# A hybrid decoder layer on one core: elementwise work moved from POOL to VectorE, two copies to ScalarE, and a new order of the heads' stage

## The chip, the cores and the metric

The kernel runs on one core of one Trainium2 chip. Five engines work side by side, each through its own queue of instructions in order: PE (TensorE) multiplies matrices, DVE (VectorE), ACT (ScalarE) and POOL (GpSimd) do elementwise work, and SP issues the transfers between HBM and the on-chip memory. The metric is the device time of one execution in microseconds (us). Engines wait for one another through semaphores, and the profile names for each wait what ended it.

## The reference, cut to what matters

The program is one layer on 1024 tokens plus 16 learned meta tokens, with 1024 channels. The part that the change touches is the mixer in the middle of the layer: four recurrent heads, and four groups of channels that are pooled over windows of 2, 4, 8 and 16 tokens.

```python
u = rmsnorm(h, mix_norm_pre[l])
proj = u @ w_in[l]
q, f_logit, i_in, g_out, v_pool, gate_a, gate_b = jnp.split(proj, cuts, axis=-1)
a = hgrn2(q, f_logit, i_in, g_out, lbs[l], hgrn_out_norm[l])
p = multiscale_pool(v_pool, pool_proj[l], pool_scale[l])
z = (jax.nn.sigmoid(gate_a) * (a @ w_branch_hgrn[l])
     + jax.nn.sigmoid(gate_b) * (p @ w_branch_pool[l]))
...
# hgrn2: f = lb + (1-lb) sigmoid(f_logit), k = (1-lb) sigmoid(-f_logit); per head and chunk of tokens
#   scores[t,s] = sum_k q[t,k] * prod(f[s+1..t],k) * k[s,k]   (s <= t)
#   o = scores @ v + (q * prod f) @ state,  state' = (prod f) * state + (k * rest of f)^T @ v
#   o is normalised per head and multiplied by sigmoid(g)
# multiscale_pool: mean over the trailing window minus the token, times a 128x128 matrix per group
```

After the mixer follow an output projection, a norm, and a gated MLP with a causal convolution. All of it is float32; the kernel splits each float32 operand into a high and a low part and makes three matrix products of them.

## The kernel before, in words

Channels lie on the 128 partitions and tokens along the free dimension. The program runs in stages: the input norm and the value projection, the other projections of the two gates and of f and q (these by a seven-product scheme, and their results go to HBM scratch: fscr, kscr, kbscr, qscr, sscr), then the heads' stage, then the branch products BB and BA, the output projection, and the MLP.

The heads' stage is the one that changes. `ORDER` writes it out by hand as a list of steps in which the engines' queues are built: `h0` to `h3` is the next step of a head, `PV0` to `PV3` the projection of a pooling group (`PVa`, `PVb` its first and second half of the contraction, names ppv), `sp` the end of the pooling of a group, `G2` and `G3` two gate projections (pg), `PP` the 128x128 product of a group (ppp), `sa` the splitting of a head's output, `w` the preparing of later weights. A tile framework then places the instructions on each engine's queue from that list; inside a queue nothing overtakes.

A head (`head_steps`) loads f, q, kb and k from scratch (L655 to L658), then builds the scores within chunks of 128 tokens by doubling: for each level 1, 2, 4 ... 64 PE multiplies k and q blocks (names sb and sl, L690, L696, L719), and VectorE grows k (L673), q (L677, L679, first step L714) and f (L681) by one level. A level's products wait for the growth of the level before it, and the growth waits for the products that still read k and q. VectorE copies the scores from PSUM: masked for small levels (L711, L721), plainly for the two large ones (L705, into sc). Then k is transposed (pt), the state increments are multiplied (ds), VectorE runs along the states (st, L768), PE multiplies the outputs (po, L785, L786), and a norm with ScalarE's logarithm and exponential (L796, L797) follows, for which the square is split into rh and rl (L836).

A weight of a projection is loaded to wraw (L147), ScalarE casts the high part (whi, L150), and another engine subtracts to get the low part (wlo, L151). There are three buffers of each of wraw, whi and wlo, and the loader runs three weights ahead (`AHEAD`), so a cast waits until PE has done with the weight three before. After a projection `post_pv` copies it to vp and makes the window sum by one to four additions of shifted rows (L818), and `pool_split` divides, subtracts and splits it (L830, plh, pll).

`POOLED` names the operations that go to POOL instead of VectorE: the first growth of k of each head (uk1), the splits of the weights of PV0 to PV3, G2, G3 and PP2, and one rl. The window sums run on POOL too. Loads of a head are issued on SP's queue after the weight load that was last created before them in the program (`tc.issue_after(stage["load"].ins)`).

Of the kernel before, what the change touches and what calls it, by code (L numbers as in the profile page):

```python
# [12 lines left out]
ALU = mybir.AluOpType  # L13

P = 128
D = 1024
SEQ = 1024
NM = 16
L = SEQ + NM
# [33 lines left out]
ZA = 4  # L53
AHEAD = 3

ORDER = ("h0 h1 PVa0 h0 h1 PVb0 h0 h1 h0 PVa1 h1 h0 sp0 PVb1 h1 h0 h1 PVa2 sp1 h0 h1 PVb2 h0 h1 h2 h0 PVa3 sp2 h1 h0 h1 h3 "
         "PVb3 h0 h1 h2 Ga2 sp3 h0 h1 h2 h3 Gb2 h2 h3 sa0 PP0 PP1 h2 h3 Ga3 h2 h3 h2 Gb3 h3 h2 h3 PP2 PP3 h2 h3 sa1 h2 h3 w0 w1 "
         "BB0 w4 h2 h3 w4 BB1 h2 h3 BB2 sa2 h3 BB3 w5 BB4 sa3 w4 w5 BB5 w5 BB6 BB7 w5 BA0 w2 BA1 w3 BA2 BA4 BA3 BA5 BA6 BA7")
POOLED = ("uk1.0 uk1.1 uk1.2 uk1.3 wBA2 wBA6 wBA7 wBB2 wPP2 wPV0 wPV1 wPV2 wPV3 wG2 wG3 "
          "rsl.0").split()  # L60
TRUNC = False

CH_ALL = [(0, 348), (348, 346), (694, 346)]
# [4 lines left out]
def trunk_kernel(ctx: ExitStack, tc: tile.TileContext, x, meta_tokens, mix_norm_pre,  # L68
# [3 lines left out]
    nc = tc.nc  # L72
    act, dve, pool_e, pe = nc.scalar, nc.vector, nc.gpsimd, nc.tensor
# [6 lines left out]
    stage = {}  # L80
# [13 lines left out]
    def nm(s):  # L94
        cnt[0] += 1
        return f"{s}_{cnt[0]}"

    def slot(n, dtype=F32, name="s"):
        return stage["fm", "p"].tile([P, n], dtype, tag="fm", name=nm(name), padded_shape=[P, LP])
# [17 lines left out]
    def small(shape, name, tag, bufs=4):  # L117
        return sm.tile(shape, F32, tag=tag, name=nm(name), bufs=bufs)
# [95 lines left out]
    class Strassen:  # L214

        ORDER = ("P1", "P2", "P6", "P5", "P3", "P7", "P4")
        MOVING = dict(P1="b11", P2="b21", P3="b22", P4="t4", P5="t1", P6="t2", P7="t3")
        SECOND = ("P3", "P5", "P7")

        def __init__(self, units, run, early, quarters, base, halo, put, whole):  # L220
# [6 lines left out]
            for u in run:  # L227
                self.seq += [(u, p) for p in self.ORDER if u >= early or p not in ("P1", "P2")]
            self.got, self.at, self.kept, self.begun = [], 0, [], {}
# [328 lines left out]
    vmd = dram.tile([NM, 512], F32, name="vmscr")  # L558
# [49 lines left out]
    def eng(op):  # L608
        return pool_e if op in POOLED else dve

# [39 lines left out]

    def head_steps(h):
        f, k, kb, q = slot(NM + L, name="f"), slot(NM + L, name="k"), slot(NM + L, name="kb"), slot(NM + L, name="q")
        vmeta = small([NM, P], "vmeta", "vmeta", 2)
        with tc.issue_after(stage["load"].ins):
            nc.sync.dma_start(f, fdr[h])  # L655
            nc.sync.dma_start(q[:, NM + T0 :], qdr[h])
            nc.sync.dma_start(kb[:, M0:], kbdr[h])
            nc.sync.dma_start(k, kdr[h])  # L658
            nc.sync.dma_start(vmeta, vmd[:, h * P : (h + 1) * P])
        yield  # L660
        pool_e.memset(f[:, NM - 1 : NM], 1.0)
        pool_e.memset(k[:, NM - 1 : NM], 0.0)
# [36 lines left out]
        def level_out(lv, ps):  # L699
            if lv >= SB:  # L700
                o3 = sc.rearrange("p (c t) -> p c t", c=NCH)
                p3 = ps[:, : NCH * lv].rearrange("p (c h) -> p c h", c=NCH)
                for i in range(P // (2 * lv)):
                    n = 2 * lv * i
                    dve.tensor_copy(o3[n : n + lv, :, n + lv : n + 2 * lv], p3[n : n + lv])  # L705
                return
            o4 = near.rearrange("p (c b two h) -> p c b two h", c=NCH, two=2, h=lv)[:, :, :, 1, :]
            p4 = ps[:, : NCH * SB // 2].rearrange("p (c b h) -> p c b h", c=NCH, h=lv)
            nb = SB // (2 * lv)
            m4 = masks[lv].rearrange("p (o b h) -> p o b h", o=1, h=lv).to_broadcast([P, NCH, nb, lv])  # L710
            dve.copy_predicated(o4, m4, p4)  # L711
# [12 lines left out]
        for lv in LEVELS:  # L724
            if lv == NM:
                pm = bank("sm")
                for i in range(HALO):
                    pe.matmul(pm[:NM, i : i + 1], k[:, i * NM : (i + 1) * NM], q[:, NM + T0 + i : NM + T0 + i + 1],
                              start=True, stop=True)
                act.copy(scm, pm[:NM, :HALO])  # L730
            ps = level_mm(lv)
            grow(lv)
            level_out(lv, ps)
            if lv == SB // 2:
                for n in range(0, P, SB):
                    act.copy(sc.rearrange("p (c t) -> p c t", c=NCH)[n : n + SB, :, n : n + SB], n3[n : n + SB])
            yield

        heads[h]["v"] = slot(NCH * P, name="vh")
        with tc.issue_after(stage["load"].ins):  # L740
            nc.sync.dma_start(heads[h]["v"].rearrange("p (c v) -> p c v", c=NCH),
                              vd[:, :, h * P : (h + 1) * P].rearrange("c p v -> p c v"))
        kt = slot(NCH * P, name="kt")
# [62 lines left out]
    def post_pv(g, pv):  # L806
        w = POOL_WINDOWS[g]
        vp, s1 = slot(L, name="vp"), slot(L, name="s1")
        s2 = slot(L, name="s2") if w > 2 else None
        for (lo, n), ps in zip(CH_ALL, pv):  # L810
            act.copy(vp[:, lo : lo + n], ps[:, :n])
        cur, step = vp, 1
        bufs = [s1, s2]
        while step < w:
            nxt = bufs[0]
            bufs = bufs[::-1]
            a = 2 * step - 1
            pool_e.tensor_tensor(nxt[:, a:L], cur[:, a:L], cur[:, a - step : L - step], ALU.add)  # L818
            cur, step = nxt, 2 * step
        pooled[g] = (cur, vp)  # L820

# [70 lines left out]
    def job(kind, i):  # L892
        if kind == "G":
            return (wblock(WIN, 0, KD, CG + i * P, P), KD, u_q, CH_Q, lambda r: post_g(i, r))
        if kind == "PV":
            return (wblock(WIN, 0, KD, CV + i * P, P), KD, u_all, CH_ALL, lambda r: post_pv(i, r))
        if kind == "PP":
            return (pool_proj[0, i].rearrange("(k c) d -> c k d", k=1), 1,
                    lambda k, lo, n: (pin[i][0][:, lo : lo + n], pin[i][1][:, lo : lo + n]), CH_Q,
                    lambda r: post_pp(i, r))  # L900
        if kind == "BA":
            return (wblock(w_branch_hgrn[0], 0, HEADS, i * P, P), HEADS, a_x, CH_Q, lambda r: post_branch(sas, i, r))
        return (wblock(w_branch_pool[0], 0, HEADS, i * P, P), HEADS, p_x, CH_Q, lambda r: post_branch(sbs, i, r))
# [4 lines left out]
    BEGUN = [(e, p) for es in ((0, 1), (2, 3, UP0)) for p in ("P1", "P2") for e in es]  # L908
    KEPT = BEGUN + [(u, p) for u in (0, UP0) for p in Strassen.ORDER[2:]]
    kept = [[dram.tile([P, 1024], F32, name=f"kept{t}{h}") for h in "hl"] for t in range(len(KEPT) // 2)]  # L910
# [54 lines left out]

    order = ORDER.split()
    order = [(o_[:-1], int(o_[-1])) for o_ in order]
# [23 lines left out]
    def gate_steps(d):  # L991
# [10 lines left out]
        else:  # L1002
# [19 lines left out]
    gates = Strassen([(WIN, dict(F=CF, Q=CQ, A=CA, B=CB)[k] + 2 * P * j) for k, j in GUNITS], range(len(GUNITS)),  # L1022
                     EARLY, gq, NM, ghalo, put_gate, lambda u, i: None)
# [116 lines left out]
    for kind, i in order:  # L1140
# [9 lines left out]
        if kind == "h":  # L1150
            if i not in gens:
                gens[i] = head_steps(i)
            next(gens[i], None)
            continue
# [36 lines left out]
    for name, names in (("v1", ("b11h", "b11l", "b21h", "b21l")), ("v2", ("b22h", "b22l", "t1h", "t1l"))):  # L1191
        n, o = (HP, HO) if name == "v1" else (HN, 0)
# [584 lines left out]
```

## Time and profile before

| | us |
|---|---|
| median of three runs | 1337.31 (1335.11 to 1337.34) |
| the profiled execution | 1336.16 |
| its span, first to last instruction | 1334.5 |
| PE busy | 1292.2 |
| VectorE busy | 972.5 |
| ScalarE busy | 519.0 |
| POOL busy | 405.2 |

The page gives per engine the time that it was busy and the number of its instructions. A group of instructions has a line of the kernel, an engine, an operation, the tile written and the tiles read, the count, the busy time, the mean of one, and the idle time of the engine just before, with what ended it. The granted clock of PE stands beside stretches of time as a share of full speed; its mean over the span is 0.988. A wait is put down to the engine that ended it last.

### The profile page before, as it was taken

The page shows a single profiled execution, that of the slowest core. Times are in us where ns is not written, and L with a number is a line of the kernel's source. Part 1 is how long each engine was busy: PE and PEld are TensorE (multiplying, and loading weights), DVE is VectorE, ACT ScalarE, POOL GpSimd, SP SyncE. Part 2 cuts the span into 40 slices and gives each one's busy share as a digit, 9 for nine tenths or more (in the row PEclk, how much of TensorE's full clock was granted, in tenths as well). Part 3 has the DMA queues.
Part 4 walks back from the last instruction along what each step waited for, and adds up shares of the span by engine and source line. Part 5 has one row for each costly group of instructions (what it writes and reads, how often), then busy time and mean ns, then how long its engine had stood idle before and what let it go on. Part 6 is the DMA issues. An engine that isn't in the chain of part 4 may idle for free.

```text
span 1334.5 us, 21944 instructions
## 1 busy us (share of the span) xinstructions
PE 1292.2 (97%) x8617; PEld 1143.3 (86%) x8617; DVE 972.5 (73%) x1287; ACT 519.0 (39%) x891; POOL 405.2 (30%) x325
## 2 busy tenths in 40 slices
PE   8999999999789879999999999999999999999997
PEld 6799899999788779987899888888888888888886
DVE  6768965542786976686668999888988885455757
ACT  5554433333125445224664222222222223454543
POOL 3015333322354100052026555446556652000000
PEclk9999999999899889999999999999999999999999
DMA  8135643334232276887686777776767799676644
GB/s 271 41 109 178 199 136 103 111 119 146 92 114 100 65 253 191 305 286 248 225 301 225 209 206 191 201 205 152 180 164 148 178 244 301 216 230 223 221 173 158
DMA packets 143802, 247.62 MB, mean 186 GB/s; under 512 B 11000, under 2 KB 75164, under 8 KB 143698
## 3 DMA queue, kind: packets, MB, share of 16 engines
q1 hardware_dynamic: 131634, 221.83, 49.4%
q0 software_dynamic: 12064, 24.38, 10.9%
q8 instruction: 68, 1.11, 0.3%
q14 instruction: 36, 0.29, 0.1%
HBM read 174.11 MB, written 95.09 MB: 202 GB/s over the span
## 4 chain that ended last, share of the span: by engine, by line
PE 62%; DVE 0%; issue 0%; ACT 0%; DMA 0%; DVEq 0%
PE P L305 11%; PE P L304 11%; PE P L307 11%; PE pd L184 5%; PE pd L185 5%; PE pd L186 5%; PE pm L184 2%; PE pm L185 2%; PE pm L186 2%; PE pba L204 1%; PE pba L205 1%; PE pba L208 1%; PE pbb L204 1%; PE pbb L205 1%; PE pbb L208 1%; PE pt L1271 1%
## 5 line engine op out<-in xcount | busy, mean ns | idle before, releaser
L305 PE MATMUL P<-v,whi 128*128 128x512 f32 (+2 forms) x408 | 140.7, 353 | 0.0
L304 PE MATMUL P<-v,whi 128*128 128x512 f32 (+2 forms) x408 | 140.7, 352 | 0.0
L307 PE MATMUL P<-v,wlo 128*128 128x512 f32 (+2 forms) x424 | 135.1, 349 | 0.0
L275 POOL TENSOR_TENSOR swa<-wraw,wraw 128x512 f32<-128x512 f32 x32 | 48.5, 1516 | 192.1 <-DMA wraw<-in_w_in_dram 98.7
L249 ACT CAST whi<-wraw 128x512 fp32r<-128x512 f32 x90 | 53.1, 618 | 102.3 <-PE P L305 75.7
L1511 DVE TENSOR_TENSOR rot<-wraw,rot 128x1024 fp32r<-128x1024 f32 x31 | 38.0, 1224 | 72.2 <-ACT rot L1510 72.2
L304 PEld LDWEIGHTS P<-v,whi 128*128 128x128 f32 x408 | 76.7, 188 | 10.4
L305 PEld LDWEIGHTS P<-v,whi 128*128 128x128 f32 x408 | 76.6, 188 | 10.2
L307 PEld LDWEIGHTS P<-v,wlo 128*128 128x128 f32 x424 | 74.1, 188 | 10.8
L185 PE MATMUL pd<-rot 128*128 128x512 f32 x272 | 82.1, 389 | 0.0
L186 PE MATMUL pd<-rot 128*128 128x512 f32 x272 | 82.1, 389 | 0.0
L184 PE MATMUL pd<-rot 128*128 128x512 f32 x272 | 81.1, 389 | 0.1
L250 DVE TENSOR_TENSOR wlo<-wraw,whi 128x512 fp32r<-128x512 f32 x86 | 77.4, 922 | 2.7 <-ACT whi L249 2.7
L250 DVE TENSOR_TENSOR wlo<-swb,whi 128x512 fp32r<-128x512 f32 x64 | 67.6, 1064 | 9.7 <-ACT whi L249 9.6
L249 ACT CAST whi<-swa 128x512 fp32r<-128x512 f32 x64 | 38.1, 618 | 92.6 <-PE P L305 77.4
L304 PE MATMUL P<-uhi,whi 128*128 128x258 f32 (+2 forms) x240 | 68.6, 303 | 0.0
L305 PE MATMUL P<-ulo,whi 128*128 128x258 f32 (+2 forms) x240 | 68.4, 303 | 0.0
L1510 ACT CAST rot<-wraw 128x1024 fp32r<-128x1024 f32 x31 | 32.7, 1054 | 90.7 <-PE pd L186 89.4
L249 ACT CAST whi<-swb 128x512 fp32r<-128x512 f32 x64 | 38.1, 618 | 70.9 <-PE P L305 61.5
L304 PE MATMUL P<-t2h,whi 128*128 128x258 f32 (+2 forms) x228 | 65.2, 304 | 0.3 <-DVE sg L864 0.3
L304 PE MATMUL P<-t4h,whi 128*128 128x258 f32 (+2 forms) x228 | 65.5, 304 | 0.0
L305 PE MATMUL P<-t4l,whi 128*128 128x258 f32 (+2 forms) x228 | 65.3, 304 | 0.0
(383 smaller groups left out, 3884.9 us busy)
## 6 DMA issues: line engine op xcount, KB each, us to landing
wraw<-in_w_in_dram SPq DMA_DIRECT2D x36, 512.0 KB, 4.8
yt<-ysum SPq DMA_DIRECT2D x33, 512.0 KB, 5.4
wraw<-in_ffn_w_gate_dram SPq DMA_DIRECT2D x26, 512.0 KB, 5.9
wraw<-in_ffn_w_up_dram SPq DMA_DIRECT2D x22, 512.0 KB, 6.5
wsum<-in_ffn_w_down_dram SPq DMA_DIRECT2D x22, 512.0 KB, 8.5
wraw<-in_w_out_dram SPq DMA_DIRECT2D x18, 512.0 KB, 5.1
ysum<-ys SPq DMA_DIRECT2D x11, 768.0 KB, 5.6
sa<-sscr SPq DMA_DIRECT2D x16, 513.0 KB, 4.4
```

What stands on the lines that cost most here:

```text
L184: pe.matmul(ps, ahi, bhi, start=first, stop=False)
L185: pe.matmul(ps, ahi, blo, start=False, stop=False)
L186: pe.matmul(ps, alo, bhi, start=False, stop=last)
L204: pe.matmul(ps[:, :n], whi[:, k, :], xhi, start=(k == 0), stop=False)
L249: act.copy(hi, src)
L250: (pool_e if 4 <= i < 2 * self.early else dve).tensor_tensor(lo, src, rr(hi), ALU.subtract)
L275: pool_e.tensor_tensor(s1, a21, a22, ALU.add)
L304: pe.matmul(d, whi[:, k, :], xh[:, c : c + w], start=(k == 0 and onto is None), stop=False, **go)
L305: pe.matmul(d, whi[:, k, :], xl[:, c : c + w], start=False, stop=False, **go)
L307: pe.matmul(x[:, o : o + w], wlo[:, k, :], xh[:, c : c + w], start=False, stop=(k == 3), **go)
L1510: act.copy(hi, src)
L1511: dve.tensor_tensor(lo, src, rr(hi), ALU.subtract)
```

## The change

All operations in `POOLED` and the window sums go from POOL to VectorE. The copies of the two large levels from PSUM to sc (L705) go from VectorE to ScalarE. The loads of heads 0 and 1 are tied to the last weight load of the stage before (`gates.loaded`) instead of the last projection weight; the small load of vmeta moves from the head's first step to the one that loads its values. `ORDER` puts the whole of PV0 and the first half of PV1 ahead of the second step of heads 0 and 1, and shifts the halves of the later projections by some places.

```diff
-ORDER = ("h0 h1 PVa0 h0 h1 PVb0 h0 h1 h0 PVa1 h1 h0 sp0 PVb1 h1 h0 h1 PVa2 sp1 h0 h1 PVb2 h0 h1 h2 h0 PVa3 sp2 h1 h0 h1 h3 "
-         "PVb3 h0 h1 h2 Ga2 sp3 h0 h1 h2 h3 Gb2 h2 h3 sa0 ...
+ORDER = ("h0 h1 PV0 PVa1 h0 h1 PVb1 h0 h1 h0 PVa2 h1 sp0 h0 h1 PVb2 h0 h1 sp1 h0 h1 h2 PVa3 h0 h1 sp2 h0 h3 "
+         "PVb3 h1 h0 h1 h0 h1 h2 Ga2 sp3 h0 h1 h2 h3 Gb2 h2 h3 sa0 ...
-POOLED = ("uk1.0 uk1.1 uk1.2 uk1.3 wBA2 wBA6 wBA7 wBB2 wPP2 wPV0 wPV1 wPV2 wPV3 wG2 wG3 "
-          "rsl.0").split()
+POOLED = ()
...
     def head_steps(h):
-        vmeta = small([NM, P], "vmeta", "vmeta", 2)
-        with tc.issue_after(stage["load"].ins):
+        with tc.issue_after((stage["load"] if h >= 2 else gates.loaded).ins):
             nc.sync.dma_start(f, fdr[h])
...
-            nc.sync.dma_start(vmeta, vmd[:, h * P : (h + 1) * P])
...
-                    dve.tensor_copy(o3[n : n + lv, :, n + lv : n + 2 * lv], p3[n : n + lv])
+                    act.copy(o3[n : n + lv, :, n + lv : n + 2 * lv], p3[n : n + lv])
...
         heads[h]["v"] = slot(NCH * P, name="vh")
+        vmeta = small([NM, P], "vmeta", "vmeta", 2)
         with tc.issue_after(stage["load"].ins):
+            nc.sync.dma_start(vmeta, vmd[:, h * P : (h + 1) * P])
...
     def post_pv(g, pv):
-            pool_e.tensor_tensor(nxt[:, a:L], cur[:, a:L], cur[:, a - step : L - step], ALU.add)
+            dve.tensor_tensor(nxt[:, a:L], cur[:, a:L], cur[:, a - step : L - step], ALU.add)
```

The framework places the rest. Lines of the changed kernel stand one to three lower in number than those of the one before in this part. Three places in the queues:

SP's queue around the first loads of heads 0 and 1; wraw_3580 (now 3486) is PV3's weight, wraw_3857 (now 3663) G2's, sscr stores are results of the gates. Before:

```order
L147 DMA wraw_3389<-in_w_in_dram 128x8x128
L659 DMA vmeta_3399<-vmscr 16x128
L659 DMA vmeta_3409<-vmscr 16x128
L871 DMA sscr<-sg_3263 128x514
L147 DMA wraw_3580<-in_w_in_dram 128x8x128
L871 DMA sscr<-sg_3321 128x512
L147 DMA wraw_3857<-in_w_in_dram 128x8x128
L871 DMA sscr<-sg_3340 128x512
L655 DMA f_3395<-fscr 128x1056
L656 DMA q_3398<-qscr 128x1026
```

Now:

```order
L146 DMA wraw_3389<-in_w_in_dram 128x8x128
L870 DMA sscr<-sg_3263 128x514
L146 DMA wraw_3486<-in_w_in_dram 128x8x128
L870 DMA sscr<-sg_3321 128x512
L146 DMA wraw_3663<-in_w_in_dram 128x8x128
L870 DMA sscr<-sg_3340 128x512
L653 DMA f_3395<-fscr 128x1056
L654 DMA q_3398<-qscr 128x1026
```

The two loads of vmeta are gone from here; the head's loads keep their place behind both weights.

VectorE's queue at the first levels of heads 0 (f_3395) and 1; sl_3592 (now 3677) is head 0's product of level 2, wlo_3666 the low part of G2's weight, s the window sums. Before:

```order
L714 TENSOR_TENSOR q_3408<-q_3408,f_3405 128x512
L681 TENSOR_TENSOR f_3395<-f_3395 128x528
L677 TENSOR_TENSOR q_3408<-q_3408,f_3405 128x1024
L721 COPY_PREDICATED near_3502<-mbase,sb_3507 128x256
L673 TENSOR_TENSOR k_3396<-k_3396,f_3395 128x264x2
L679 TENSOR_TENSOR q_3398<-q_3398,f_3395 128x256x2
L711 COPY_PREDICATED near_3457<-mask_145,sl_3592 128x64x2
```

Now:

```order
L674 TENSOR_TENSOR q_3406<-q_3406,f_3403 128x1024
L718 COPY_PREDICATED near_3585<-mbase,sb_3590 128x256
L678 TENSOR_TENSOR f_3395<-f_3395 128x528
L678 TENSOR_TENSOR f_3403<-f_3403 128x528
L150 TENSOR_TENSOR wlo_3666<-wraw_3663,whi_3665 128x1024
L670 TENSOR_TENSOR k_3396<-k_3396,f_3395 128x264x2
L676 TENSOR_TENSOR q_3398<-q_3398,f_3395 128x256x2
L708 COPY_PREDICATED near_3540<-mask_145,sl_3677 128x64x2
L817 TENSOR_TENSOR s_473_3670<-vp_3669 128x1039
```

The split of G2's weight and a window sum of group 1 stand now between the growth steps; on PE both sb products come after twelve of sixteen k steps of PV0 and PV1, where they came within PV0.

VectorE's queue at the states (st) of heads 0 and 1, after the last growth; s_500_4129 is group 2's window sum, vp_4282 of the changed kernel group 3's projection. Before:

```order
L714 TENSOR_TENSOR q_4166<-q_4166,f_4163 128x512
L830 SCALAR_TENSOR_TENSOR s_500_4129<-s_500_4129,vp_4128 128x1026
L836 TENSOR_TENSOR pll_4233<-s_500_4129,plh_4232 128x1026
L151 TENSOR_TENSOR wlo_4344<-wraw_4341,whi_4343 128x128
L768 SCALAR_TENSOR_TENSOR st_4255<-st_4255,f_3395,ds_4259 128x128 x4
L768 SCALAR_TENSOR_TENSOR st_4255<-st_4255,f_3395,ds_4268 128x128
L768 SCALAR_TENSOR_TENSOR st_4275<-st_4275,f_3405,ds_4279 128x128
```

Now:

```order
L817 TENSOR_TENSOR s_526_4283<-vp_4282 128x1039
L817 TENSOR_TENSOR s_527_4284<-s_526_4283 128x1037
L670 TENSOR_TENSOR k_4233<-k_4233,f_4232 128x528
L817 TENSOR_TENSOR s_526_4283<-s_527_4284 128x1033
L817 TENSOR_TENSOR s_527_4284<-s_526_4283 128x1025
L828 TENSOR_SCALAR s_527_4284<-c_566_4501 128x1
L829 SCALAR_TENSOR_TENSOR s_527_4284<-s_527_4284,vp_4282 128x1026
L767 SCALAR_TENSOR_TENSOR st_4313<-st_4313,f_3395,ds_4317 128x128 x2
```

Group 3's sums, the mean and the first growth of head 3's k stand ahead of the states, where before the states came first and the sums ran on POOL.

More of the change, by code (lines that the diff above doesn't have):

```diff
@@ L54 @@
 AHEAD = 3
-ORDER = ("h0 h1 PVa0 h0 h1 PVb0 h0 h1 h0 PVa1 h1 h0 sp0 PVb1 h1 h0 h1 PVa2 sp1 h0 h1 PVb2 h0 h1 h2 h0 PVa3 sp2 h1 h0 h1 h3 "
-         "PVb3 h0 h1 h2 Ga2 sp3 h0 h1 h2 h3 Gb2 h2 h3 sa0 PP0 PP1 h2 h3 Ga3 h2 h3 h2 Gb3 h3 h2 h3 PP2 PP3 h2 h3 sa1 h2 h3 w0 w1 "
+ORDER = ("h0 h1 PV0 PVa1 h0 h1 PVb1 h0 h1 h0 PVa2 h1 sp0 h0 h1 PVb2 h0 h1 sp1 h0 h1 h2 PVa3 h0 h1 sp2 h0 h3 "
+         "PVb3 h1 h0 h1 h0 h1 h2 Ga2 sp3 h0 h1 h2 h3 Gb2 h2 h3 sa0 PP0 PP1 h2 h3 Ga3 h2 h3 h2 Gb3 h3 h2 h3 PP2 PP3 h2 h3 sa1 h2 h3 w0 w1 "
          "BB0 w4 h2 h3 w4 BB1 h2 h3 BB2 sa2 h3 BB3 w5 BB4 sa3 w4 w5 BB5 w5 BB6 BB7 w5 BA0 w2 BA1 w3 BA2 BA4 BA3 BA5 BA6 BA7")
-POOLED = ("uk1.0 uk1.1 uk1.2 uk1.3 wBA2 wBA6 wBA7 wBB2 wPP2 wPV0 wPV1 wPV2 wPV3 wG2 wG3 "
-          "rsl.0").split()
+POOLED = ()
 TRUNC = False
```

## The prediction

> **What bounds the kernel now.** I read the page's engine totals first, then stretches of the span between 327 us, where the heads' stage begins, and 585 us, where its last branch product ends, then who PE waited for there.
>
> ```profile
> PE 1292.2 (97%) x8617; PEld 1143.3 (86%) x8617; DVE 972.5 (73%) x1287; ACT 519.0 (39%) x891; POOL 405.2 (30%) x325
> ```
>
> PE is busy for 97% of the span, so only its 42 idle us and its slow-clock time can be won. In the stretches the columns are busy us of PE, PEld, DVE, ACT and POOL, then PE's granted clock, DMA share and GB/s:
>
> ```profile
> 344.00:371.00 27.00, 20.79 (x636) 19.93 (x627) 21.81 (x30) 3.32 (x7) 8.20 (x4) 0.82 0.05 12
> 371.00:385.00 14.00, 14.00 (x139) 13.53 (x138) 12.01 (x22) 4.89 (x12) 3.03 (x4) 0.89 0.08 24
> 430.00:445.00 15.00, 8.49 (x276) 7.85 (x277) 14.68 (x20) 10.62 (x18) 3.88 (x2) 0.77 0.17 47
> 475.00:512.00 37.00, 34.11 (x226) 33.27 (x227) 23.99 (x42) 19.25 (x28) 0.00 (x0) 0.93 0.75 242
> 512.00:585.00 73.00, 73.00 (x461) 73.00 (x460) 52.28 (x83) 20.34 (x35) 6.36 (x4) 1.00 0.79 281
> ```
>
> From 512 us on PE never stops; before, it does, and its clock falls with it. PE's waits from 327 to 512 us (total, times, longest):
>
> ```profile
> PE sl L696 <- DVE q L677: 5.5, 1, 5.5
> PE ds L765 <- DMA vh<-vscr: 4.2, 1, 4.2
> PE sl L696 <- DVE q L679: 4.0, 4, 2.6
> PE sb L719 <- DVE q L714: 3.7, 1, 3.7
> PE sl L696 <- issue: 3.0, 1, 3.0
> PE po L785 <- ACT rs L796: 2.9, 1, 2.9
> ```
>
> With eight smaller ones they make 29.8 us; most end with VectorE's growth of q and k (L714, L677, L679). Slow clock adds 20.79 x 0.18 + 14.00 x 0.11 + 8.49 x 0.23 + 34.11 x 0.07 = 9.6 us. Some 39 us is the ceiling of any gain here.
>
> **The change part by part.** First VectorE's own account. The rows pair a VectorE step with what POOL ran beside it:
>
> ```profile
> 334.35 0.69 DVE L714 TENSOR_TENSOR q<-q,f 128x512 f32<-128x512 f32 x1 [7.54 <-DMA q<-qscr]
> 336.42 1.23 DVE L677 TENSOR_TENSOR q<-q,f 128x1024 f32<-128x1024 f32 x1 [1.38 <-PE sb L719]
> 340.49 2.34 POOL L151 TENSOR_TENSOR wlo<-wraw,whi 128x1024 fp32r<-128x1024 f32 x1 [1.15 <-ACT whi L150]
> 340.63 2.76 DVE L714 TENSOR_TENSOR q<-q,f 128x512 f32<-128x512 f32 x1 [2.60 <-DMA q<-qscr]
> 439.79 0.72 DVE L681 TENSOR_TENSOR f<-f 128x528 f32<-128x528 f32 x1
> 379.86 0.68 DVE L673 TENSOR_TENSOR k<-k,f 128x512 f32<-128x512 f32 x1
> ```
>
> The same L714 step takes 0.69 us alone and 2.76 us when POOL's L151 started 0.14 us earlier. All thirteen slowed steps of the stage lie beside a two-operand POOL instruction. By groups, 326 to 512 us (count, busy us, mean ns):
>
> ```profile
> L679 DVE TENSOR_TENSOR q<-q,f 128x512 f32<-128x512 f32 x24 | 22.0, 918 | 0.0
> L673 DVE TENSOR_TENSOR k<-k,f 128x512 f32<-128x512 f32 x12 | 12.4, 1037 | 2.8 <-PE sl L690 2.1 <-PE sl L696 0.6
> L677 DVE TENSOR_TENSOR q<-q,f 128x1024 f32<-128x1024 f32 x4 | 8.8, 2203 | 5.7 <-PE sb L719 5.7
> L673 DVE TENSOR_TENSOR k<-k,f 128x528 f32<-128x528 f32 x12 | 8.5, 710 | 5.2 <-PE sm L728 3.7 <-PE sl L696 1.5
> L681 DVE TENSOR_TENSOR f<-f 128x528 f32<-128x528 f32 x4 | 6.1, 1527 | 0.0
> L836 DVE TENSOR_TENSOR rl<-rs,rh 128x1026 fp32r<-128x1026 f32 x3 | 5.8, 1935 | 2.5 <-ACT rh L835 2.5
> L714 DVE TENSOR_TENSOR q<-q,f 128x512 f32<-128x512 f32 x4 | 5.8, 1441 | 10.6 <-DMA q<-qscr 10.6
> L836 DVE TENSOR_TENSOR pll<-s,plh 128x1026 fp32r<-128x1026 f32 x4 | 4.9, 1229 | 5.5 <-ACT plh L835 5.5
> L161 DVE TENSOR_TENSOR wlo<-wraw,whi 128x1024 fp32r<-128x1024 f32 x4 | 4.9, 1222 | 3.2 <-DMA kept6l<-wlo 2.2 <-ACT whi L160 0.9
> L705 DVE COPY sc<-sl 32x256 f32<-32x256 f32 x8 | 3.3, 414 | 0.1
> L705 DVE COPY sc<-sl 64x512 f32<-64x512 f32 x4 | 2.7, 677 | 0.0
> ```
>
> Relief: 24 x (918 - 680) + 12 x (1037 - 680) + 4 x (2203 - 1230) + 4 x (1527 - 720) + 4 x (1441 - 690) + 3 x (1935 - 1229) ns (L679 by L673's price, of the same shape) = 5.7 + 4.3 + 3.9 + 3.2 + 3.0 + 2.1 = 22.2 us. Added: six weight splits of 128x1024 at 1.22, ten window sums of at most 128x1039 (nearest row L836, 1.23), four first k steps at 0.71, one rl at 1.23, one small split at 0.3: 7.3 + 12.3 + 2.8 + 1.2 + 0.3 = 23.9 us. Gone to ScalarE: 3.3 + 2.7 = 6.0 us. Net: 4.3 us less on VectorE. The prices of window sums and copies lie between this row and, if VectorE ran them as slowly as the slowed steps, 2.2 us each; I take the row, since nothing on POOL but memsets is left beside them.
>
> So the balance hardly moves; the order decides. I followed it by adding these durations (each VectorE step costs about 0.1 us less from start to start) along the new queues. Rows for PE's steps and the places I compare with:
>
> ```profile
> 325.73 0.42 SPq L655 DMA_DIRECT2D f<-fscr  x1
> 326.95 0.40 PE L204 MATMUL ppv<-uhi,whi 128*128 128x348 f32 x1 [0.88 <-DVE sg L862]
> 328.46 0.33 PE L204 MATMUL ppv<-uhi,whi 128*128 128x348 f32 x1
> 334.20 0.33 PE L204 MATMUL ppv<-uhi,whi 128*128 128x348 f32 x1
> 371.15 0.49 PE L204 MATMUL ppv<-uhi,whi 128*128 128x346 f32 x1
> 365.14 0.70 PE L696 MATMUL sl<-q,k 128*32 128x16 f32 x62
> 402.44 1.72 PE L765 MATMUL ds<-vh,kt 128*128 128x128 f32 x14
> 414.42 0.76 PE L719 MATMUL sb<-q,kb 128*32 128x32 f32 x64
> 427.75 1.06 ACT L797 ACTIVATE rs<-rs 128x1026 f32<-128x1026 f32 x1
> 437.75 1.05 PE L696 MATMUL sl<-q,k 128*32 128x16 f32 x64 [5.52 <-DVE q L677]
> 474.98 3.33 PE L765 MATMUL ds<-vh,kt 128*128 128x128 f32 x14 [4.15 <-DMA vh<-vscr]
> ```
>
> The loads: nothing. In SP's queue the first head's f still stands behind all five weight loads and behind the store before it; only two small vmeta loads left. It issues at 325.7 us as now, and q of head 1 lands at 340.6.
>
> More projection first: 8 us. A k step of a projection (nine matmuls) takes (334.20 - 328.46) / 4 = 1.435 us. Twelve of them before the two sb products (0.7 each, by the 414.42 row), and four after, keep PE at work from 326.95 until 351.3, across the waits for q (3.7, 3.0 and 0.5 us) and their slow clock. VectorE has both heads' q ready by 348.3.
>
> Splits in VectorE's queue: back 2 us here. The split of G2 stands before the level-2 growth. It needs ScalarE's cast, which needs the buffer of PV1's weights, free when PE ends PV1 at 351.3: cast done 352.4, split 353.5, growth of k and q 354.8. PE, ready at 352.7, waits 2.1 us; behind it wait both heads' levels. PV2's first half, head 1's level 4 and head 0's level 8 are then done by 363.7; the kernel now comes to the same place at 365.14, but without that half of 5.7 us, so it is 7 us behind. Two more waits, 2.3 and 1.7 us before the 32-row levels, stand against 2.6 and 1.5 us now; all of PV3 and the transposes end at 393.2 instead of 402.4: ahead 9.2.
>
> Window sums ahead of the states: back 3 us. Group 3's four sums and two steps of head 3 and the mean stand on VectorE before the fourteen state updates. They start when PV3's copies end (393.3) and take 0.1 + 2 x 0.62 + 5 x 1.14 + 0.1 = 7.1 us: 400.4. PE, through with the state products at 396, waits 4.5 us for the first state; the outputs end at 408.5 against 414.4: ahead 5.9.
>
> No contention in the norm chain: 5 us. There rl took 3.35 and q's step of head 3 took 3.36 us beside POOL; at 1.23 each, and with ScalarE's first exponential at 419 instead of 427.75, head 3's level 2 runs at 426.5 instead of 437.75: ahead 11.
>
> Copies on ScalarE and two more splits: back 2.7 us. Before the cast whose store stands ahead of head 2's value load in SP's queue ScalarE now does two copies (0.75 + 0.6), and VectorE two splits (1.1 + 0.2). PE's wait for that load (474.98) ends at about 466.5. Everything later in the stage hangs on this and moves with it; after it PE is full, so 8.5 us reach the end.
>
> The profiled execution took 1336.16 us for its span of 1334.5; less 8.5 is 1327.7. The median of the runs is 1.15 us above it: 1328.8, which I round to **1328.5**.
>
> On the clock I charged each new wait of over 2 us with slow matmuls behind it, some 3 us in all, because a wait of 2.6 us is followed by 0.49 us matmuls at 371.15 where 0.33 is usual. The Trainium skill ("TensorE: Matmul & The Clock Gate", "What's actually happening") has the clock fall only after a window of about 3.4 us without work. By it the 2.1 and 2.3 us waits would be free and the sum near 1326; this trace does not agree, by that 0.49.
>
> **The rivals.**
> More comes through. Splits and sums hold PE less than I add up, as when ScalarE's cast comes earlier: the 2.1 and 4.5 us waits and their slow clock (1.5) vanish, 8.1 us more: 1320. For it: PE's other work was ordered around them. Against: each split follows a buffer that PE frees late.
> The gain is given back. PE's 4.2 us wait for head 2's values is set by transfers, with DMA at 0.75 there. If that load, queued behind stores and weight loads, lands no earlier, all that was won before it is a longer wait: 1336.5. Against: each of these issues follows a compute step that comes earlier.
> Slower: VectorE becomes the bound. It is already at 14.68 of 15 us from 430 to 445. If its slow steps are not POOL's doing, the relief of 22.2 stays out and it carries 17.9 us more; less the 8 us that the projections hide, 9.9 us on the path: 1347. It decides once less than 13.7 of the 22.2 us comes (8.5 short). Against: thirteen of thirteen coincidences.
> The change does not do what it says for the loads; that is in the forecast already.
>
> **How the numbers follow.** Forecast 0.61 (own range 1322 to 1334), more 0.16, given back 0.13, slower 0.10. Below 0.2% (2.7 us) nothing can be told from no change, so faster begins at 1334.6: 0.58 of the first, all 0.16 and 0.04 of the third make 0.78; same 0.12; slower 0.10. The range leaves out the slow case and the end of the second: 1319 to 1337.
>
> **What would show it.** Right: no slowed L714, L677 or L679 (means near 0.69, 1.23 and 0.69 us); head 0's f still issued at 325.7; PE without a gap until 351, then one of about 2 us at the first levels behind the split, and one of 4 to 5 us at the first output behind the state update; the state products' wait for vh at 466 to 467. Wrong: PE's total wait above 25 us in the stage, or a later wait for vh.

## The result and the profile after

The change takes 1327.2 us (median of four, 1325.76 to 1327.77); the kernel before takes 1336.45 us beside it (four, 1335.11 to 1337.34). The ratio is 0.993, with a 95% interval of 0.9913 to 0.9947: faster by about 9 us, where 1328.5 us had been forecast. The profiled execution took 1327.77 us with a span of 1326.0, 8.5 us shorter than the span before. The page's busy totals of the changed kernel:

```profile
PE 1292.2 (97%) x8617; PEld 1144.3 (86%) x8617; DVE 964.4 (73%) x1297; ACT 524.2 (40%) x903; POOL 356.7 (27%) x303
```

PE does the same work; POOL lost 48.5 us and VectorE did not gain them, it lost 8.1. The stretches of the heads' stage (columns as in the prediction: PE, PEld, DVE, ACT, POOL, granted clock, DMA share, GB/s):

```profile
344.00:371.00 27.00, 24.74 (x620) 23.63 (x620) 20.96 (x35) 3.32 (x7) 0.00 (x0) 0.94 0.08 22
371.00:385.00 14.00, 10.05 (x231) 9.79 (x231) 13.19 (x22) 7.84 (x20) 0.85 (x5) 0.76 0.89 307
430.00:445.00 15.00, 11.60 (x219) 11.05 (x220) 13.95 (x28) 3.70 (x11) 0.00 (x0) 0.89 0.37 108
475.00:512.00 37.00, 37.00 (x254) 36.31 (x254) 24.26 (x39) 23.02 (x32) 0.00 (x0) 1.00 0.56 193
```

PE now has no gap and full clock from 475 us on, where it had 34.11 busy us of 37 at 0.93. What it waited for between 327 and 512 us (total, times, longest):

```profile
PE ds L764 <- DMA vh<-vscr: 6.9, 2, 5.2
PE sl L693 <- DVE q L676: 3.9, 2, 2.0
PE sl L687 <- DVE q L676: 3.5, 2, 2.1
PE sl L693 <- issue: 2.4, 2, 2.1
PE sl L687 <- ACT sc L702: 1.9, 1, 1.9
...
PE pt L750 <- DVE plo L842: 0.8, 1, 0.8
```

All nine groups add to 21.6 us, against 29.8 before. Two things in this list matter for what follows: the load of vh is the largest wait now, and the wait of 2.9 us for ScalarE's logarithm (`PE po L785 <- ACT rs L796` before) is no longer there. The groups of VectorE and ScalarE that answer to those of before, 326 to 512 us (count, busy us, mean ns):

```profile
L676 DVE TENSOR_TENSOR q<-q,f 128x512 f32<-128x512 f32 x24 | 16.4, 684 | 0.0
L670 DVE TENSOR_TENSOR k<-k,f 128x512 f32<-128x512 f32 x12 | 8.2, 686 | 4.4 <-PE sl L687 2.8 <-PE sl L693 1.5
L674 DVE TENSOR_TENSOR q<-q,f 128x1024 f32<-128x1024 f32 x4 | 4.9, 1220 | 1.1 <-PE sb L716 1.1
L711 DVE TENSOR_TENSOR q<-q,f 128x512 f32<-128x512 f32 x4 | 2.8, 689 | 6.2 <-DMA q<-qscr 6.2
L678 DVE TENSOR_TENSOR f<-f 128x528 f32<-128x528 f32 x4 | 2.7, 701 | 0.0
L817 DVE TENSOR_TENSOR s<-vp 128x1039 f32<-128x1039 f32 x4 | 5.0, 1246 | 0.6 <-ACT scm L727 0.6
L702 ACT COPY sc<-sl 32x256 f32<-32x256 f32 x8 | 2.9, 362 | 1.5 <-PE sl L687 1.4
```

Every slowed step is back at the price of its undisturbed neighbours: L679 918 to 684 ns, L673 1037 to 686, L677 2203 to 1220, L681 1527 to 701, L714 1441 to 689 (now L676, L670, L674, L678, L711). The places that the prediction followed, from the timelines of SP, PE and VectorE (start, us, what it waited for):

```profile
325.35 0.42 SPq L653 DMA_DIRECT2D f<-fscr  x1
354.50 0.63 PE L693 MATMUL sl<-q,k 128*32 128x16 f32 x52 [2.03 <-DVE q L676]
374.69 0.70 PE L687 MATMUL sl<-q,k 128*32 128x32 f32 x32 [2.10 <-DVE q L676]
377.24 1.07 PE L687 MATMUL sl<-q,k 128*32 128x32 f32 x32 [1.85 <-ACT sc L702]
395.57 0.33 SPq L146 DMA_DIRECT2D wraw<-in_pool_proj_dram  x1
396.20 0.37 SPq L740 DMA_DIRECT2D vh<-vscr  x1
396.48 1.83 PE L764 MATMUL ds<-vh,kt 128*128 128x128 f32 x14
400.41 1.80 PE L764 MATMUL ds<-vh,kt 128*128 128x128 f32 x14 [1.69 <-DMA vh<-vscr]
402.14 0.38 PE L777 MATMUL po<-scm,vmeta 16*128 16x2 f32 x2
402.91 3.95 DVE L767 SCALAR_TENSOR_TENSOR st<-st,f,ds 128x128 f32<-128x128 f32 x14
410.29 0.76 PE L716 MATMUL sb<-q,kb 128*32 128x32 f32 x64
428.69 0.73 PE L693 MATMUL sl<-q,k 128*32 128x16 f32 x64 [2.13 <-issue]
462.41 0.48 SPq L740 DMA_DIRECT2D vh<-vscr  x1
469.12 3.33 PE L764 MATMUL ds<-vh,kt 128*128 128x128 f32 x14 [5.17 <-DMA vh<-vscr]
493.49 0.49 PE L784 MATMUL po<-sc,vh 128*128 128x128 f32 x2
```

So the lead over the kernel before is 4.1 us at the end of the outputs (414.42 to 410.29), 9.1 us at head 3's level 2 (437.75 to 428.69), 5.9 us at the wait for vh (474.98 to 469.12), and 8.5 us at the end.

### The profile page after: what moved, and what is told of

Same layout as the page of the kernel before. It is cut to its first block, busy times and chain, and to the rows that moved or that the text cites. A ratio compares the mean times of both kernels' runs of the same rounds, so it can differ in the third digit from the quotient of the medians.

```text
span 1326.0 us, 21946 instructions
## 1 busy us (share of the span) xinstructions
PE 1292.2 (97%) x8617; PEld 1144.3 (86%) x8617; DVE 964.4 (73%) x1297; ACT 524.2 (40%) x903; POOL 356.7 (27%) x303
## 4 chain that ended last, share of the span: by engine, by line
PE 94%; issue 2%; ACT 2%; DMA 1%; DVE 1%; SPq 0%; DVEq 0%; ACTq 0%
PE P L303 17%; PE P L304 17%; PE P L306 17%; PE pd L183 5%; PE pd L184 5%; PE pd L185 5%; PE pm L183 2%; PE pm L184 2%; PE pm L185 2%; PE pbb L203 1%; PE pbb L204 1%; PE pbb L207 1%; PE pba L203 1%; PE pv L184 1%; PE pba L204 1%
## 5 line engine op out<-in xcount | busy, mean ns | idle before, releaser
L249 DVE TENSOR_TENSOR wlo<-wraw,whi 128x512 fp32r<-128x512 f32 x86 | 73.3, 875 | 2.7 <-ACT whi L248 2.7
```

The lines of the kernel that those rows point to most:

```text
L249: (pool_e if 4 <= i < 2 * self.early else dve).tensor_tensor(lo, src, rr(hi), ALU.subtract)
```

## The experiments

The theory was: POOL's two-operand instructions block VectorE's, which costs PE its waits; the order alone hides only the first waits; the loads of the first heads do nothing; the wait for vh then limits what comes through. The rivals: VectorE's slow steps have another cause and VectorE becomes the bound; the copies or the loads carry the gain. All results, each against the kernel before on the same chip. "Stage" is the time from the first product of PV0 to the first of BA (names ppv and pba) in the profiled execution, 213.9 us before and 205.9 us with the change:

| run | what it is | median us (n) | ratio, 95% interval | stage us |
|---|---|---|---|---|
| e1_order_only | before, new order alone | 1330.15 (4) | 0.9947, 0.9932 to 0.9962 | 206.6 |
| e2_engines_only | before, engines alone | 1328.42 (4) | 0.9928, 0.9911 to 0.9946 | 206.5 |
| e5_sums_on_pool | change, sums back on POOL | 1336.87 (10) | 0.9999, 0.9989 to 1.0009 | 217.0 |
| e6_pooled_on_pool | change, list `POOLED` back | 1331.64 (6) | 0.9961, 0.9947 to 0.9974 | 210.1 |
| e3_loads_as_before | change, loads back | 1327.0 (4) | 0.9917, 0.9899 to 0.9936 | 204.1 |
| e4_copies_on_dve | change, copies back | 1330.12 (4) | 0.9939, 0.9922 to 0.9956 | 208.0 |
| e8_vh_at16 | change, vh of heads 2, 3 earlier | 1325.22 (4) | 0.9899, 0.9879 to 0.9919 | 201.9 |
| e9_g3_sums_late | change, group 3's sums later | 1331.4 (4) | 0.9946, 0.9927 to 0.9965 | 209.2 |
| e11_old_order_vh16 | e8 with the old order | 1322.83 (4) | 0.9894, 0.9878 to 0.991 | 199.1 |
| e12_vh_all16 | change, all four vh earlier | 1322.87 (4) | 0.9893, 0.9878 to 0.9908 | 199.4 |
| e15_vh16_po_later | e8, head 3's outputs later | 1323.75 (4) | 0.9898, 0.9882 to 0.9915 | 202.3 |
| e17_h3_before_norm1 | e12, head 3 ahead of head 1's norm | 1322.03 (5) | 0.9887, 0.9869 to 0.9905 | 196.5 |

The kernel before had a median of 1336.94 us beside e1, e2, e5 and e6, 1337.83 beside e3, e4, e8 and e9, 1336.75 beside e11, e12 and e15, and 1338.3 beside e17, so the ratios are what to compare across rows. From the first product of BA to the end every profile takes 793.5 to 795.2 us: all but 1.7 us of the differences are made within the stage.

**Either half alone.** The order on the old engines, and the engines in the old order:

```diff
# e1_order_only, against before
-ORDER = ("h0 h1 PVa0 h0 h1 PVb0 h0 h1 h0 PVa1 ...
+ORDER = ("h0 h1 PV0 PVa1 h0 h1 PVb1 h0 h1 h0 PVa2 ...
# e2_engines_only, against before
-POOLED = ("uk1.0 uk1.1 uk1.2 uk1.3 wBA2 ...
+POOLED = ()
-                    dve.tensor_copy(o3[n : n + lv, ...
+                    act.copy(o3[n : n + lv, ...
-            pool_e.tensor_tensor(nxt[:, a:L], ...
+            dve.tensor_tensor(nxt[:, a:L], ...
```

> The kernel before with the new ORDER alone; POOL keeps its 22 operations, VectorE its copies, the loads stay. My theory (order and relief both pay): the projections cover the first waits for q as in the change (the 3.7, 3.0 and 0.5 us waits gone), but VectorE's steps beside POOL stay slow (L679 mean about 0.9 us, L677 about 2.2), so the late gain of the norm chain (5 us) stays out: about 1330.5. Rival A (the order is all of it): 1327. Rival B (the relief is all of it): 1336.

> The kernel before with all two-operand work on VectorE and the two copies on ScalarE, old ORDER, old loads. My theory: no slow step is left (L679 mean 0.69, L677 1.23, first q step 0.69), the 5.5 us wait of head 3 shrinks to 2 or less, the early waits for q stay at 4 to 5 us in all: about 1332.5. Rival A (order is all): 1336.5. Rival B (relief is all): 1327. If the slow steps are not POOL's doing, VectorE carries 17.9 us more and it comes out at 1345 or more.

The order alone gives 6.8 us, near what was expected of it; the engines alone give 8.5 us, 4 us more than expected; both give 9.3 us: they do not add. PE's waits from 327 to 512 us add to 23.1 us in e1, 21.5 in e2 and 21.6 in the change. Of e1:

```profile
PE ds L765 <- DMA vh<-vscr: 5.9, 2, 4.1
PE sl L696 <- ACT sg L622: 4.6, 1, 4.6
```

Of e2:

```profile
PE ds L764 <- DMA vh<-vscr: 5.1, 1, 5.1
PE po L784 <- ACT rs L795: 2.6, 1, 2.6
```

The two halves work at different places. The order alone takes away the waits around the first q (7.3 us before, 3.7 and 3.0 us the largest) and brings one of 2.85 us behind them. At head 3's level 2 it leaves 4.6 of the 5.5 us. The profile puts that wait down to ScalarE, but VectorE's q step took 3.37 us there beside POOL and ended at 431.15 us, 0.10 us before the product began; of e1, POOL, VectorE and PE:

```profile
427.56 2.51 POOL L151 TENSOR_TENSOR wlo<-wraw,whi 128x1024 fp32r<-128x1024 f32 x1 [8.56 <-ACT whi L150]
427.78 3.37 DVE L677 TENSOR_TENSOR q<-q,f 128x1024 f32<-128x1024 f32 x1
431.25 1.06 PE L696 MATMUL sl<-q,k 128*32 128x16 f32 x64 [4.61 <-ACT sg L622]
```

The engines alone leave 4.2 us of waits around the first q and 2.3 us at head 3's level 2. From the stage's first product to the end of the wait for vh the order alone saves 6.3 us, the engines alone 10.3, both together only 5.5; behind it the order saves 1.0 us, the engines lose 2.9, both together save 2.5. What the new order costs beside the moved engines up to there, no run takes apart. e2 issues the load of vh at 458.26 us, 4.1 us ahead of the change, and loses this behind it: by the wait at the outputs, and by a granted clock of 0.66 in the ten microseconds around it:

```profile
490.00:500.00 10.00, 8.03 (x42) 8.06 (x43) 5.87 (x9) 5.66 (x8) 0.00 (x0) 0.66 0.41 116
```

The rival that VectorE's slow steps have another cause falls here: e2 keeps the old order, and its means of the steps that were L681 and L677 are 718 and 1220 ns, against 1527 and 2203.

**What POOL's instructions cost.** The window sums, and then the list `POOLED`, go back to POOL:

```diff
# e5_sums_on_pool, against the change
-            dve.tensor_tensor(nxt[:, a:L], ...
+            pool_e.tensor_tensor(nxt[:, a:L], ...
# e6_pooled_on_pool, against the change
-POOLED = ()
+POOLED = ("uk1.0 uk1.1 uk1.2 uk1.3 wBA2 wBA6 wBA7 wBB2 wPP2 wPV0 wPV1 wPV2 wPV3 wG2 wG3 "
+          "rsl.0").split()
```

> The changed kernel with the ten window sums back on POOL. They free VectorE of 12.4 us and bring back ten slow stretches of about 2.2 us. My theory (the relief pays): VectorE's two-operand steps beside them take 2 to 3 us again, and the time is 1 to 4 us over the change: about 1330. Rival (VectorE's load is what binds, the contention is small): 2 to 4 us under it, about 1324.

> The changed kernel with the operations of POOLED (six large splits, one small, four first k steps, one rl) back on POOL; the window sums stay on VectorE. My theory: VectorE loses 12 us of work and gets some eight slow steps back, the split of G2 no longer stands between the growth steps (the 2.0 us wait at the first levels goes), the rl of head 0 costs 2 us of the norm chain: 1 to 4 us over the change, about 1330. Rival (VectorE's load binds): 2 to 4 us under the change, about 1324.

With only the ten sums on POOL the whole gain, 9 us, is gone (1336.87, ratio 0.9999), though VectorE is freed of ten instructions of some 1.24 us; both expectations missed this. The timelines of POOL, VectorE and PE of e5 show how:

```profile
353.69 1.92 POOL L817 TENSOR_TENSOR s<-vp 128x1039 f32<-128x1039 f32 x1 [8.72 <-ACT vp L810]
355.68 2.26 POOL L817 TENSOR_TENSOR s<-s 128x1037 f32<-128x1037 f32 x1
...
353.74 2.43 DVE L670 TENSOR_TENSOR k<-k,f 128x528 f32<-128x528 f32 x1
356.09 2.40 DVE L676 TENSOR_TENSOR q<-q,f 128x512 f32<-128x512 f32 x1
...
358.63 1.05 PE L693 MATMUL sl<-q,k 128*32 128x16 f32 x64 [5.47 <-DVE q L676]
```

POOL's first sum ends at 355.61; VectorE's k step, begun 0.05 us after it, ends at 356.17, its own 0.6 us later. POOL's second ends at 357.94, VectorE's q step at 358.49. So the step seems not to run slower beside POOL but to run after it. The two steps take 1.73 and 1.71 us more than their 0.70 and 0.69 us in the change, 3.4 us together, and PE's wait is longer by as much: 5.47 us for 2.03. The Trainium skill ("SBUF — State Buffer", "Who interferes with whom") says that a VectorE instruction with two SBUF inputs contends with a GpSimd instruction that reads SBUF, over a shared pair of ports that one of them holds as a lock; these rows agree with it. This profile is the slowest of e5's ten times (1340.41), so its stage overstates the median's loss.

But 9 us is not a price of ten sums wherever they stand. Of the 11.1 us of stage that this profile loses against the change, 3.3 lie behind the wait for vh, where a wait of 3.0 us for the logarithm is back, which hangs on a buffer, as told under e8. And e1, measured beside e5, has the same ten sums on POOL and the list `POOLED` too (its copies and loads as before), with eleven slowed VectorE steps for e5's six, and takes 6.7 us less. At the first levels e5 has the split of G2's weight on VectorE ahead of the two slowed steps; e1 has it on POOL and waits 2.85 us there for 5.47. What a slowed step costs depends on what else stands in VectorE's queue.

In e6 the stage is some 4 us longer than the change's. The first level waits 2.8 us instead of 2.0, head 3's level 2 waits 4.6 instead of 2.1, and 3.2 us of wait for the logarithm are back at head 3's outputs, whose place is told under e8; the waits of 1.53 and 1.87 us that follow in the change shrink to 0.98, 2.4 us in all. Without the wait for the logarithm, less than 1 us of stage is left to this list beside the new order, so it does its harm at few places.

**The loads and the copies.** Each of the two undone alone:

```diff
# e3_loads_as_before, against the change
-        with tc.issue_after((stage["load"] if h >= 2 else gates.loaded).ins):
+        vmeta = small([NM, P], "vmeta", "vmeta", 2)
+        with tc.issue_after(stage["load"].ins):
...
+            nc.sync.dma_start(vmeta, vmd[:, h * P : (h + 1) * P])
# e4_copies_on_dve, against the change
-                    act.copy(o3[n : n + lv, ...
+                    dve.tensor_copy(o3[n : n + lv, ...
```

> The changed kernel with the loads of heads 0 and 1, and vmeta's, as before. My theory (the loads are worth nothing): the same as the change within 0.1%, about 1327; head 0's f is issued at the same 325 us. Rival (the loads carry part of the gain): 1329 or more.

> The changed kernel with the twelve copies of the two large levels back on VectorE. By my sum (two copies on ScalarE ahead of the cast whose store stands before head 2's value load cost 1.35 us) that load is issued up to 1.35 us earlier, while VectorE has 6 us more over the stage: about 1327, PE's 1.9 us wait for the ScalarE copy at 377 us gone. Rival (VectorE's load is on the path): 1330 or more.

The loads are worth nothing that can be measured (1327.0, its interval overlapping the change's). With the copies back on VectorE the time came at the rival's, not the expected one: each of its four times lies above each of e3's, which ran beside it (3.1 us between the medians). Against the change, the ratio is 0.0009 worse, 1.2 us, with overlapping intervals; its profile's stage is 2.1 us longer, of which 1.5 us is the wait for the logarithm at the outputs, and the 1.85 us wait before the 32-row level stays, now for VectorE's q. So the copies gain some 1 to 3 us, and in the profiles more by which instruction the outputs wait for than by VectorE's balance.

**The sums ahead of the states.** The prediction charged 3 us for group 3's window sums standing before the state updates. Here they go behind, into `pool_split`:

```diff
# e9_g3_sums_late, against the change; window_sums(g) is the loop of post_pv
+        if g < HEADS - 1:
+            window_sums(g)
...
     def pool_split(g):
+        if g == HEADS - 1:
+            window_sums(g)
```

> The changed kernel with group 3's four window sums moved from the end of its projection to the step that splits them, so that they stand behind the state updates of heads 0 and 1 on VectorE. By my prediction (PE waits 4.5 us for the first state behind the sums, 3 us of it on the path): 1324. By the trace of the change, where PE's wait there is 1.7 us and for a value load: the same as the change, 1327.

Both expectations were wrong: 1331.4, slower than the change by 0.0016 in the ratio, the intervals overlapping, and by 3.3 us of stage; each of its four times lies above each of e3's beside it. The states come at once and head 1's wait for vh is gone. The sums now stand in the norm chain, and the split of group 3 that follows them (`pll`, at 428.19 us for 417.78) among the growth steps of heads 2 and 3:

```profile
415.92 3.77 DVE L823 TENSOR_TENSOR s<-s 128x1037 f32<-128x1037 f32 x3 [2.12 <-PE ms L793]
428.04 1.05 PE L693 MATMUL sl<-q,k 128*32 128x16 f32 x64 [3.30 <-ACT sg L621]
```

Head 3's level 2 still begins a little earlier than in the change, 428.04 us for 428.69, though PE waits 3.30 us for it and not 2.13. The loss comes behind it: a further wait of 2.8 us, a granted clock of 0.65 for 0.89 from 430 to 445 us, and 2.0 us for VectorE's sa at head 3's outputs. The place that I had priced as a loss is, in this profile, the better one.

**The wait for vh.** The largest wait left is for the value loads of heads 2 and 3, which are written into the program when k is transposed. They are issued four steps earlier, then for all heads:

```diff
# e8_vh_at16, against the change; load_v() holds slot, vmeta and both loads
+            if h >= 2 and lv == 16:
+                vmeta = load_v()
...
-        heads[h]["v"] = slot(NCH * P, name="vh")
-        vmeta = small([NM, P], "vmeta", "vmeta", 2)
...
+        if h < 2:
+            vmeta = load_v()
# e12_vh_all16, against e8
-            if h >= 2 and lv == 16:
+            if lv == 16:
...
-        if h < 2:
-            vmeta = load_v()
# e11_old_order_vh16, against e8
-ORDER = ("h0 h1 PV0 PVa1 h0 h1 PVb1 h0 h1 h0 PVa2 ...
+ORDER = ("h0 h1 PVa0 h0 h1 PVb0 h0 h1 h0 PVa1 ...
# e15_vh16_po_later, against e8
-         "... BB1 h2 h3 BB2 sa2 h3 BB3 w5 ...
+         "... BB1 h2 BB2 h3 sa2 BB3 h3 w5 ...
```

> The changed kernel with the loads of the values (vh) and vmeta of heads 2 and 3 created four steps earlier in the program, so that they stand in SP's queue ahead of the stores of kept weights. If PE's 5.2 us wait at 469 us and the slow clock behind it (some 2 to 3 us) come only from the place of that load, about 1320. Rival (the next wait, for ScalarE's copies of the transposes or for VectorE, takes its place): 1325 or more.

> The changed kernel with the value loads of heads 2 and 3 four steps earlier, and one branch product (BB2) put between head 2's norm and head 3's outputs, and the next (BB3) ahead of head 3's norm. If the 2.0 us wait of head 3's output for ScalarE's logarithm and the slow clock behind it (0.64 us matmuls in place of 0.39) are what ate the gain of the early load: 1322. If head 3's later norm then holds up the branch products of the heads: 1326 or more.

> The changed kernel with the value loads of all four heads created four steps earlier. Beside the run with heads 2 and 3 alone (1325.2), the 1.5 us wait of head 1's state products goes. If what is won before 430 us still reaches the end: 1323.5. If the wait at head 3's output (2.0 us there) takes it: 1325.

> The changed kernel (engines and loads) with the ORDER of before, and the value loads of heads 2 and 3 created four steps earlier. With the old order alone the engines' part was 4 us ahead of the change at those loads and lost it at a 2.6 us wait of head 3's output for ScalarE and the slow clock behind it. If that wait is a floor that ScalarE's chain sets by itself, a PE that comes earlier only waits longer there: 1325. If it moves with PE's work, as everything before it did: 1321.

e8 takes the whole wait of 5.17 us away. It gains 2 to 4 us: 1.8 against e3, which ran beside it and differs from the change only in the loads, 4.1 by the ratios against the change (0.993 to 0.9899), whose intervals overlap. PE in e8:

```profile
463.73 1.83 PE L771 MATMUL ds<-vh,kt 128*128 128x128 f32 x14
...
487.12 0.38 PE L784 MATMUL po<-scm,vmeta 16*128 16x2 f32 x2 [2.01 <-ACT rs L802]
...
575.98 0.47 PE L183 MATMUL pm<-whi,zc 128*128 128x512 f32 x1 [1.40 <-ACT zc L1139]
```

PE reaches head 3's outputs earlier and waits there 2.01 us for ScalarE; a further wait of 1.40 us comes later. In e15, which places these outputs behind a branch product, that product waits instead (`PE pbb`, 2.76 us for the same logarithm). The 2.9 us wait of the kernel before and those of e2, e4, e5 and e6 are of the same kind. In the kernel before, ScalarE and PE:

```profile
498.05 1.99 ACT L160 CAST whi<-wraw 128x1024 fp32r<-128x1024 f32 x2 [4.00 <-issue]
500.06 1.28 ACT L796 ACT_TABLE_LOAD   x1
501.36 1.42 ACT L796 ACTIVATE rs<-ms,eps_t 128x342 f32<-128x342 f32 x3
...
501.95 0.49 PE L785 MATMUL po<-sc,vh 128*128 128x128 f32 x2 [2.89 <-ACT rs L796]
```

The product reads nothing that the logarithm writes. It resumes 0.12 us after the first of the three ends (501.36 plus a third of 1.42), which fits a PSUM buffer that this logarithm still reads. PE's instructions there are the same in both kernels; the semaphores on which they wait are not. Of the kernel before, then of the change (PE's queue, with the waits):

```
L778 MATMUL po_5478<-scm_4584,vmeta_4299 128x2 [waits DVE_49]
L785 MATMUL po_5481<-sc_4582,vh_5248 128x128 [waits Activation_49]

L777 MATMUL po_5478<-scm_4580,vmeta_5247 128x2 [waits DVE_49]
L784 MATMUL po_5481<-sc_4578,vh_5246 128x128 [waits DVE_49,Pool_49]
```

The framework gave the tile a PSUM buffer that had another last reader. In the built program of the kernel before, po_5481 lies in PSUM bank 5, last held by ms_5461, which this logarithm reads (L796, `rs<-ms`); in the change it lies in bank 7, last held by pbb_5408, which VectorE's sa reads (L879). In the kernels that keep these outputs at this place, where one of the first two output products waits on ScalarE's semaphore, PE waits 1.4 to 3.2 us there for the logarithm (before, e2, e4, e5, e6, e8, e11, e12, e17); where both wait only on VectorE's and POOL's, it never waits for it (the change, e3, e1, e9; the last two wait 1.1 and 2.0 us for VectorE's sa). In all nine of the first kind, in their built programs, that product's bank was last read by the logarithm; in the four of the second kind the bank of the sc product was last read by sa. So the cause of this wait is read from the programs, over 13 kernels; what it is worth by itself is not shown, as no run changed the buffer alone.

e12 also takes head 1's wait of 1.69 us away; at 0.9893 it lies below the change's interval, but not measurably below e8. e11, the same loads as e8 but the old order, takes 1322.83: beside the engines' move and earlier values the new order gives nothing that can be measured.

**The best version.** In e12 PE still waits 2.3 us at head 3's level 2. Moving head 1's norm behind the steps of heads 2 and 3:

```diff
# e17_h3_before_norm1, against e12
-         "... sp3 h0 h1 h2 h3 Gb2 ...
+         "... sp3 h0 h2 h3 h1 Gb2 ...
```

> The changed kernel with all four value loads early (as in the run of 1322.9) and head 2's first level and head 3's first products ahead of head 1's norm in ORDER, so that head 3's first growth of q no longer stands on VectorE behind head 1's o, which waits for ScalarE's exponential. If that place is what PE's 2.3 us wait at head 3's level 2 (427.8 us) comes from, the wait goes and some 2 us reach the end: 1321. If the late stage (head 3's output behind ScalarE's logarithm) sets the end anyway: 1323.

That wait is gone, and the next level waits 1.97 us for a weight's split. The median, 1322.03, cannot be told from e12's. But its interval, 0.9869 to 0.9905, lies below the change's, 0.9913 to 0.9947: about 0.4% faster than the change and 1.1% faster than the kernel before. Its profile is the fastest of its five times (1318.06).

## Why the prediction was right, point by point

**VectorE's relief** held in each row, and the balance too: VectorE's busy time from 326 to 512 us went from 134.73 to 130.61 us, 4.1 less where 4.3 were worked out. The window sums cost 1.25 us at most, for the 1.23 of the row taken. e2, where no slowed step is left, and the rows of e5 show that POOL's instructions are the cause.

**The loads: nothing.** f is issued at 325.35 for 325.73, with a stage that begins 0.37 us earlier; e3 confirms it.

**More projection first** held: PE has no wait until 352.5, and the waits for the first q are gone. What did not hold is that "the order decides": e2, in the old order, is 8.3 us ahead of the kernel before at the first state products (394.14 for 402.44), the change 6.0 (396.48), and in e11 against e8 the new order gives nothing either.

**Splits in VectorE's queue.** The wait of 2.1 us behind the split of G2 came as 2.03, and those before the 32-row levels as 2.10 and 1.85 for 2.3 and 1.7. The lead that was to follow was too large: the transposes ended at 396.1, not 393.2. Slow products took some 1.3 us after the first wait and 2.1 us after the pair, 3.4 in this part alone where 3 were charged for the whole stage; the rest I can't itemise.

**Sums ahead of the states.** The wait of 4.5 us for the first state, named as a sign of being right, did not occur. PE was later than worked out: the state products took 4.4 us for the 2.8 given, and 1.69 us more went to head 1's vh, whose load stands in SP's queue behind a small weight load (395.57, 396.20) and which the prediction never looked at. VectorE's updates began at 402.9, for 400.4, and PE, at its first output at 402.1, did not have to wait for them. The outputs ended at 410.3, for 408.5; and e9 shows that the alternative place is no gain.

**The norm chain** gave 5 us as said (from 4.1 to 9.1), from a lead 1.8 us smaller.

**Copies and splits before the load of vh** gave back 3.2 us for 2.7. The wait for vh ended at 469.1, for 466.5: a lead of 5.9, for 8.5.

**"After it PE is full, so 8.5 us reach the end"** is the step that failed. The lead at vh was 2.6 us too large, and behind it the kernel before was not full: the 2.9 us wait for the logarithm, quoted among the waits but given no price, vanished. 5.9 + 2.9 = 8.8, against 8.5 in the spans; 0.4 of the 5.9 was there when the stage began. Two terms mis-sized by nearly the same amount made the total come out. That is luck: the second hangs on a PSUM buffer that no line of the diff mentions. (The sum itself came to 1328.8; 1328.5 is not its rounding.)

**The rivals.** "Given back at vh" was partly true: PE's wait there grew from 4.15 to 5.17 us, though the load is issued 6.8 us earlier. Taking it away (e8) is worth 2 to 4 us of its 5.2. "VectorE becomes the bound" is refuted by e2 and e5.

## What to carry to other kernels

A dependent chain on VectorE should have no two-operand POOL work beside it: steps of 0.7 us took 2.4 us there. What that costs depends on where the slowed steps stand: ten sums on POOL took 9 us from the changed kernel, though they free 12.4 us of VectorE, while the new order with all 22 operations on POOL (e1) is only 2 to 3 us behind the change. Cures need not add (6.8 and 8.5 us alone, 9.3 together), and a wait taken away is worth only what the next one in line leaves: 5.2 us of wait gave 2 to 4. Before a wait is taken as fixed, compare on which semaphore the same instruction waits in both kernels; buffers handed out by a framework can change it.

## What the runs showed that I had not expected

A stall of 2 us slows PE's clock in one execution and not in another of nearly the same program. The run e3 and the change wait 1.95 and 2.03 us at the first level, and 2.01 and 2.13 us at head 3's level 2. The stretches behind these two waits (granted clock third from the end), of e3:

```profile
355.00:357.00 2.00, 1.94 (x72) 1.81 (x64) 2.00 (x4) 0.00 (x0) 0.00 (x0) 1.00 0.78 232
430.00:432.00 2.00, 2.00 (x9) 2.00 (x8) 2.00 (x3) 1.69 (x5) 0.00 (x0) 0.50 0.00 1
```

Of the change:

```profile
355.00:357.00 2.00, 1.77 (x31) 1.63 (x20) 2.00 (x4) 0.00 (x0) 0.00 (x0) 0.61 0.71 210
430.00:432.00 2.00, 2.00 (x15) 2.00 (x14) 2.00 (x3) 1.88 (x6) 0.00 (x0) 1.00 0.00 0
```

Nor does the length decide within these few hundredths: at the first level e12 falls behind a wait of 1.94 us (0.77 from 355 to 357 us, then 0.50), and e17 keeps 1.00 behind 1.99. Behind the pair of 2.10 and 1.85 us (1.81 in e3) the clock was 0.50 from 378 to 380 us in the change, e3, e4, e8, e9 and e15 alike. The Trainium skill ("TensorE: Matmul & The Clock Gate", "What's actually happening") describes a free-running window of about 3.4 us over which PE's activity is watched, which agrees with a fall that depends on where in it a wait lies; no run here shows the window itself. It lets the clock fall only after a whole idle window, and with that this case does not agree: 2.03 us were enough. So the prediction's charge for every wait over 2 us was too regular; it is a chance of a few microseconds, not a price.
